# A four-layer-norm hybrid encoder on one core: GpSimd broadcasts the mLSTM's running maxima, a head's normalisation changes place, and the first and last pieces are cut smaller

## The chip, the core and the metric

The kernel runs on one core of one Trainium2 chip. The core has five engines that run side by side and wait for each other by semaphores: TensorE (PE, matrix products into PSUM; its weight loads are shown as PEld), VectorE (DVE), ScalarE (ACT), GpSimd (POOL) and SyncE (SP, which here only starts DMAs). The metric is the device time of one execution in microseconds (us). All times of instructions below are counted from the start of the profiled span.

## What is computed

The input is x, 256 tokens by 1024 features, float32. Two macaron layers follow each other; each is a SwiGLU block, a mixer and a second SwiGLU block, every one behind a residual with a factor and a layer norm:

```python
x = layer_norm(ALPHA * x + 0.5 * swiglu(x, w_in, w_out), g, b)
x = layer_norm(ALPHA * x + mixer(x), g, b)      # layer 0: mLSTM, layer 1: windowed attention
x = layer_norm(ALPHA * x + 0.5 * swiglu(x, w_in2, w_out2), g, b)
```

The mLSTM has 4 heads and runs in both directions over the tokens. In the reference it goes chunk by chunk; written out over all 256 tokens, direction d of head h weights the product of query t and key s by exp(u[s] - m[t]), where u is the input gate less the cumulated log forget gate and m[t] is the running maximum of u up to t (from the other end in the second direction). Sums of these weights, bounded below, divide the result; the two directions are added, each head is normalised over its 256 features, and a sigmoid gate and an output product follow. In 32-bit precision the kernel computes every product as three: each operand is split in a high part that TensorE takes exactly (float32r) and the rest, and high x high, high x low and low x high are added.

## The kernel before

**Stages.** Six stages run in order: ffn, mlstm, ffn, ffn, attn, ffn (the list `stages`, line 329). Tokens are handled as two tiles t of 128. `xt[t]` holds a token tile, `xT` its transpose in high and low parts.

**Weights.** The class `Weights` (line 147) streams all weights through a ring. A "word" is one load of 128x1024 floats by SP into `w_raw` (or `s_raw`), a "piece" is a word split by ACT into `w_hi` (`high`, line 214) and by DVE into `w_lo` (`low`, line 238). The ring has 10 pieces; `take` hands them out, `done` frees those used and lets the next ones be split. In the ffn stages the class `Paced` (line 52) keeps a running estimate of each engine's time and puts splits between the matmuls by it; in the mixers the places of the splits are written out by hand (`spare`, `W.done(0, n)`, lists such as `MP`). All engines work through their instructions in the program's order. Since every operation of PE, DVE and ACT passes through one helper, the profile shows them all under line 138; tiles tell them apart.

**Begin.** `ffn` with `start` (line 604) issues 14 transposes of the identity (`warm`), transposes the first half of `xt[0]` in 4 blocks into a PSUM bank `py`, splits it (DVE makes the high part there), splits piece 0 in two halves of 512 columns, and issues 8 more identity transposes. `first_mm` (line 629) then multiplies piece 0 and piece 1 in an order of its own.

**mLSTM.** `mlstm` (line 867) projects values, then gates. DVE makes the rows `cum`, `u` and the running maxima `pm` by scans (up to line 936). ACT and DVE split `pm` into `pn` (high part in partitions 0 to 63, low part in 64 to 127). In the loop over m and g (line 978) the queries and keys are projected, and after each of the four products `weights(h)` (line 961) makes the weights of one head: two matmuls of a column of `neg_id` with `pn` put -m[t] of each direction on all 128 partitions of a PSUM bank, ACT makes six exponentials of 128x128 from it with `u` as bias, and POOL sets the wrong side of the diagonal to zero by two selects. Then, for each head, `scores` multiplies queries, keys and weights, `mix` multiplies the result with the values, `divide` (line 1029) divides: ACT scales the first direction, DVE scales and adds the second. `combine` takes the head's mean and variance on DVE and lets POOL raise the variance to the power -1/2; `settle` (line 1054) subtracts and scales on DVE. `gate_out` multiplies by the sigmoid. The order of the heads is written out at line 1078: scores(h) with combine(h-2) inside, mix(h-1), divide(h-1), settle(h-2).

**End.** `tail` (line 559) ends every stage: all products of token tile 0, then tile 1. For tile 1 the output half o=1 does its first half of products, o=0 all, o=1 the rest (`order`, line 574). `Norm.half` adds a 512-column half to the residual and takes its statistics (`bn_stats`), `Norm.finish` aggregates them, lets POOL raise the variance to -1/2, and applies the norm in two DVE passes; in the last stage both go in cuts of 512 columns, and SP stores each cut.

Of the kernel before, what the change touches and what calls it, by code (L numbers as in the profile page):

```python
# [16 lines left out]
D = 1024  # L17
# [129 lines left out]
class Weights:  # L147
# [66 lines left out]
    def high(self):  # L214

        nc, i = self.nc, self.made
        p = self.plan[i]
        while self.half and (p["word"] not in self.raw or any(h[0] == p["needs"] for h in self.half)):
            self.low()
        while any(s_[0] == p["needs"] or p["word"] not in self.raw for s_ in self.sums):  # L220
            self.sum()
        if p["word"] not in self.raw:
            return False
        scale, raw = p["scale"], self.raw[p["word"]]
        hi = self.pool.tile([128, D], FR, name="w_hi", tag="w_hi", bufs=RING)
        if i == 0:
            for j in range(2):
                s_ = slice(j * 512, j * 512 + 512)
                nc.scalar.copy(hi[:, s_], raw[:, s_])
        elif scale is None:  # L230
            nc.scalar.copy(hi, raw)
        else:
            nc.scalar.activation(hi, raw, AF.Copy, scale=scale())
        self.half.append((i, hi))
        self.made += 1
        return True

    def low(self):
# [5 lines left out]
        lo = self.pool.tile([128, D], FR, name="w_lo", tag="w_lo", bufs=RING)  # L244
        if i == 0:
# [75 lines left out]
def trunk_kernel(ctx: ExitStack, tc: tile.TileContext, x, ffn_w_in, ffn_w_out, ln_g, ln_b, ml_w_in, ml_gate_b,  # L321
# [67 lines left out]
    for j, (kind, l, i, _) in enumerate(stages):  # L389
        if kind == "ffn":  # L390
# [7 lines left out]
            for c0 in (0, F):  # L398
                for a in range(4):
                    wide(wi, a * 256, c0)  # L400
            for g in range(GROUPS):
# [59 lines left out]
    neg_sink = consts.tile([128, 16], F32, name="neg_sink")  # L461
    neg_id = consts.tile([128, 64], FR, name="neg_id")

    def small_loads():
# [8 lines left out]
        nc.gpsimd.tensor_scalar(neg_sink, sink, -1.0, None, op0=OP.mult)  # L473
        nc.vector.scalar_tensor_tensor(neg_id, ident[:, 0:64], -1.0, ident[:, 64:128], op0=OP.mult, op1=OP.subtract)

# [52 lines left out]
    class Norm:  # L528
        def __init__(self, t, ca, eps, gb, last=False):
            self.t, self.ca, self.eps, self.gb, self.last = t, ca, eps, gb, last  # L530
            self.stats = state.tile([128, 2, 6], F32, name="stats", tag="stats", bufs=2)

        def half(self, h, y):
            z = xt[self.t][:, h * 512:(h + 1) * 512]
            nc.vector.scalar_tensor_tensor(z, z, self.ca, y, op0=OP.mult, op1=OP.add)
            nc.vector.bn_stats(self.stats[:, h], z)

        def finish(self, spare):
            mv = state.tile([128, 2], F32, name="mv", tag="mv", bufs=2)
            nc.vector.bn_aggr(mv, self.stats)  # L540
            rs = state.tile([128, 2], F32, name="rs", tag="rs", bufs=2)
# [7 lines left out]
            if len(cuts) == 1:  # L549
                W.done(0, spare)  # L550
            for s_ in cuts:
                nc.vector.scalar_tensor_tensor(z[:, s_], z[:, s_], rs[:, 1:2], self.gb[1][:, s_],
                                               op0=OP.mult, op1=OP.add)
                if self.last:
                    nc.sync.dma_start(out[0, tok(self.t), s_], z[:, s_])
            if len(cuts) > 1:
                W.done(0, spare)

    def tail(y, h, todo, first, norm, last, turn_at, between=None):

        def one(t, o, n):
            c, (i, w) = todo[t][n]
            mm3(y[t][o], h(c, t), pair(w, A, 0, slice(o * 512, o * 512 + 512)), first and n == 0, n == len(todo[t]) - 1)

# [11 lines left out]
        for j, (o, n) in enumerate(order):  # L576
            if j == full + turn_at:
                emit_x(0, last)
            one(1, o, n)
            if j >= half and (n < half) == (o == 0):  # L580
                W.done(todo[1][n][1][0] + 1, next(more))
            if n == full - 1:
                norm[1].half(o, y[1][o])
        norm[1].finish(1)
        W.done(most=TD[bound[0]])
# [6 lines left out]
    def ffn(l, i, n, pending, last):  # L592
        with ExitStack() as ph:
# [35 lines left out]
            def first_mm(ps, a):  # L629

                def mm(t, i, j):
                    for k in (2 * a, 2 * a + 1):
                        nc.tensor.matmul(ps[t], xT[i][:, k, tok(t)], pieces[a][j][:, k % 2], start=i == j == k == 0,
# [233 lines left out]
    def mlstm(l, n, pending, last):  # L867
        with ExitStack() as ph:
# [92 lines left out]
            def weights(h):  # L961
                w = tile_([128, 2, 3, 128], F32, "wt", bufs=4)
                pb = wbank((128, 2, S))
                for d in range(2):
                    r = 32 * d + h
                    sel = neg_id[:, r:r + 1].to_broadcast([128, 128])
                    nc.tensor.matmul(pb[:, d], sel, pn, start=True, stop=True)
                for sb in range(2):
                    nc.scalar.activation(w[:, 0, sb], pb[:, 0, tok(sb)], AF.Exp, bias=ucol[:, sb, h:h + 1])
                    nc.scalar.activation(w[:, 1, sb], pb[:, 1, tok(sb)], AF.Exp, bias=ucol[:, sb, 32 + h:33 + h])  # L970
                nc.scalar.activation(w[:, 0, 2], pb[:, 0, tok(1)], AF.Exp, bias=ucol[:, 0, h:h + 1])
                nc.scalar.activation(w[:, 1, 2], pb[:, 1, tok(0)], AF.Exp, bias=ucol[:, 1, 32 + h:33 + h])
                for d in range(2):
# [104 lines left out]
            for h in range(4):  # L1078
# [332 lines left out]
```

## Time and profile before

| what | value |
| --- | --- |
| median of 3 runs | 927.92 us (927.56 to 928.36) |
| the profiled execution itself | 928.32 us |
| its span, first to last instruction | 926.6 us |
| outside the span | 1.72 us |
| mean granted TensorE clock | 0.997 |
| PE / DVE / ACT / POOL busy | 99% / 85% / 59% / 11% of the span |
| DMA, mean over the span | 202 GB/s |

The profile is read by engines. A row of the timeline gives start, time, engine, line, operation, what it writes and reads, its shape and how many follow each other; in brackets the idle time of the engine just before and what ended it. A matmul row's end is modelled: matmuls overlap, and the distance between two starts tells what one costs. Where equal instructions are merged, the time is that from the first start to the last end.

### The profile page before, as it was taken

How to read it: one execution, taken by the hardware profiler on the slowest of the kernel's cores; microseconds unless marked ns; L12 is line 12 of the kernel's file. 1: busy time of each engine (PE TensorE's matmuls, PEld its weight loads, DVE VectorE, ACT ScalarE, POOL GpSimd, SP SyncE). 2: the span in 40 equal slices, each digit the busy share in tenths (PEclk: the TensorE clock that was granted, in tenths of full speed). 3: DMA queues.
4: the chain of work that ended last, by engine and by line, in shares of the span. 5: the costliest groups of instructions: out<-in, count | busy, mean ns of one | idle time of the engine just before them, and what ended most of it. 6: DMA issues, size and time to landing. Idle time of an engine off the chain costs nothing.

```text
span 926.6 us, 12512 instructions
## 1 busy us (share of the span) xinstructions
PE 916.5 (99%) x4506; PEld 767.3 (83%) x4506; DVE 785.4 (85%) x948; ACT 544.4 (59%) x766; POOL 98.1 (11%) x144
## 2 busy tenths in 40 slices
PE   9999999999999999999999999999999999999996
PEld 7888888889988888888888888888888888888885
DVE  5899997886699799988887899988868878998875
ACT  5656756347664548565636566565569555757460
POOL 0010103011111010101010101010435300110100
PEclk9999999999999999999999999999999999999998
DMA  8979774646535949685558597737434385969421
GB/s 280 356 180 334 216 246 74 229 133 199 188 108 188 344 112 345 166 304 137 160 176 323 144 330 210 269 69 227 156 122 133 101 273 195 274 194 346 122 86 45
DMA packets 98461, 187.54 MB, mean 202 GB/s; under 512 B 6720, under 2 KB 37456, under 8 KB 98400
## 3 DMA queue, kind: packets, MB, share of 16 engines
q1 hardware_dynamic: 91072, 173.04, 54.7%
q0 software_dynamic: 6752, 12.66, 8.6%
q10 hardware_dynamic: 576, 1.05, 0.3%
q8 instruction: 35, 0.57, 0.2%
q14 instruction: 26, 0.21, 0.1%
HBM read 185.68 MB, written 1.05 MB: 202 GB/s over the span
## 4 chain that ended last, share of the span: by engine, by line
PE 87%; DVE 8%; ACT 2%; issue 2%; DMA 1%; POOL 0%; SPq 0%; DVEq 0%; ACTq 0%; POOLq 0%
PE pw L138 56%; PE py L138 30%; DVE w_lo L138 3%; DMA s_raw<-in_ffn_w_in_dram 1%; DVE x L138 1%; ACT w_hi L138 1%; DVE s_raw L138 1%; DVE h L138 1%; DVE stats L138 0%; DVE wt L138 0%; ACT h L138 0%; DVE a_lo L138 0%; DVE hst L138 0%; DVE e L138 0%; DVE S L138 0%
## 5 line engine op out<-in xcount | busy, mean ns | idle before, releaser
L138 DVE TENSOR_TENSOR w_lo<-w_raw,w_hi 128x1024 fp32r<-128x1024 f32 (+1 forms) x237 | 281.8, 1219 | 24.7 <-ACT w_hi L138 22.4
L138 ACT CAST w_hi<-w_raw 128x1024 fp32r<-128x1024 f32 (+1 forms) x237 | 241.7, 1050 | 81.7 <-PE py L138 27.1
L138 PE MATMUL pw<-w_hi,xT_hi 128*128 128x512 f32 x560 | 221.6, 397 | 0.0
L138 PE MATMUL pw<-w_hi,xT_lo 128*128 128x512 f32 x560 | 218.0, 390 | 0.0
L138 PE MATMUL pw<-w_lo,xT_hi 128*128 128x512 f32 x560 | 217.4, 390 | 0.0
L138 ACT CAST w_hi<-s_raw 128x1024 fp32r<-128x1024 f32 x144 | 148.1, 1052 | 80.6 <-DVE s_raw L138 44.0
L138 DVE TENSOR_TENSOR w_lo<-s_raw,w_hi 128x1024 fp32r<-128x1024 f32 x144 | 173.0, 1220 | 22.4 <-ACT w_hi L138 21.9
L138 PE MATMUL py<-w_hi,h_hi 128*128 128x512 f32 x352 | 138.0, 392 | 0.0
L138 PE MATMUL py<-w_lo,h_hi 128*128 128x512 f32 x352 | 137.1, 390 | 0.0
L138 PE MATMUL py<-w_hi,h_lo 128*128 128x512 f32 x352 | 137.1, 390 | 0.0
L138 PEld LDWEIGHTS pw<-w_hi,xT_lo 128*128 128x128 f32 x560 | 105.0, 188 | 22.4
L138 PEld LDWEIGHTS pw<-w_lo,xT_hi 128*128 128x128 f32 x560 | 105.3, 188 | 21.0 <-DVE w_lo L138 0.4
L138 PEld LDWEIGHTS pw<-w_hi,xT_hi 128*128 128x128 f32 x560 | 105.0, 188 | 20.2 <-ACT xT_hi L138 0.2
L138 DVE TENSOR_TENSOR s_raw<-s_raw 128x1024 f32<-128x1024 f32 x72 | 87.2, 1221 | 1.0
L267 POOL DMA_DIRECT2D s_raw<-in_ffn_w_in_dram x24 | 29.2, 1215 | 511.8 <-DVE w_lo L138 469.4
L138 PEld LDWEIGHTS py<-w_hi,h_lo 128*128 128x128 f32 x352 | 66.1, 188 | 13.9
L138 PEld LDWEIGHTS py<-w_lo,h_hi 128*128 128x128 f32 x352 | 66.1, 188 | 13.8 <-DVE w_lo L138 0.3
L138 PEld LDWEIGHTS py<-w_hi,h_hi 128*128 128x128 f32 x352 | 66.1, 188 | 13.5
L138 PE MATMUL pw<-w_hi,S_hi 128*128 128x512 f32 x192 | 74.7, 389 | 0.0
L138 PE MATMUL pw<-w_lo,S_hi 128*128 128x512 f32 x192 | 74.7, 389 | 0.0
L138 PE MATMUL pw<-w_hi,S_lo 128*128 128x512 f32 x192 | 74.7, 389 | 0.0
L138 DVE TENSOR_TENSOR h_lo<-pw,h_hi 128x512 fp32r<-128x512 f32 x44 | 30.2, 688 | 24.4 <-ACT h_hi L138 24.3
(206 smaller groups left out, 1087.6 us busy)
## 6 DMA issues: line engine op xcount, KB each, us to landing
w_raw<-in_ffn_w_out_dram SPq DMA_DIRECT2D x88, 512.0 KB, 5.2
s_raw<-in_ffn_w_in_dram SPq DMA_DIRECT2D x72, 512.0 KB, 6.2
w_raw<-in_ffn_w_in_dram SPq DMA_DIRECT2D x56, 512.0 KB, 5.2
w_raw<-in_ffn_w_in_dram SPq DMA_DIRECT2D x96, 256.0 KB, 4.2
s_raw<-in_ffn_w_in_dram POOLq DMA_DIRECT2D x24, 512.0 KB, 6.0
w_raw<-in_ml_w_in_dram SPq DMA_DIRECT2D x24, 512.0 KB, 4.6
w_raw<-in_at_w_in_dram SPq DMA_DIRECT2D x12, 512.0 KB, 4.7
w_raw<-in_ml_w_out_dram SPq DMA_DIRECT2D x8, 512.0 KB, 4.0
```

Source lines behind the costliest of these rows:

```text
L138: r = f(out, *args, **kw)
L267: nc.gpsimd.dma_start(t.rearrange("p (k f) -> p k f", k=self.words[w]["k"]), v, accum_op=OP.add)
```

## The change

1. The mLSTM's maxima. `neg_id`, `pn` and the two matmuls per head go. Two DMAs issued by POOL copy the rows of `pm` to partitions 0, 32, 64, 96 of a new tile `most`; in `weights(h)` two POOL instructions `partition_broadcast` put each direction's row of 256 floats on all 128 partitions of the tile `wt`, in SBUF. ACT's six exponentials read that tile with scale -1 and write it in place, direction 0 first. In the built program POOL also gets an instruction that loads another instruction library ahead of the first broadcast and one that loads the usual one again after the last select.
2. A head's normalisation. `divide` takes a function `between`, called after ACT's scaling and before DVE's scale and add. `settle(h-2)` is called there instead of after `divide(h-1)`; the same for `settle(2)`, which now stands inside `divide(3)`, ahead of `combine(3)`.
3. The end. In the last stage's tile 1, half o=1 ends its first half of products with a sum of its own (`first`: residual plus sum, no statistics). The rest of that half is done in two quarters of 256 columns, each in its own PSUM bank; `quarter` adds and takes statistics of 256 columns. The last pass of the norm goes in cuts of 512, 256 and 256 columns, and ACT's queue instead of SP's issues the last store.
4. The begin. Word 0 is loaded by two DMAs of 256 KB. The first two 128-column blocks of `xt[0]` are transposed on their own into a bank `pw` and split first; the first four are then transposed into the bank `py` (of which blocks 2 and 3 are split, ACT making the high part), 6 identity transposes follow instead of 8. Piece 1 is also split in halves. `first_mm` uses piece 0 block by block, with the transposes of `xt[1]` after its first matmul instead of its second.

Apart from these places the order of instructions on every engine stays the same.

```diff
@@ high, low
-        if i == 0:
+        if i < 2:
...
@@ plan
-                    wide(wi, a * 256, c0)
+                    if j == c0 == a == 0:
+                        piece([two(wi, 0, 0)[:, k:k + 1] for k in range(2)], 2)
+                    else:
+                        wide(wi, a * 256, c0)
...
@@ class Norm
+        def first(self, h, y):
+            z = xt[self.t][:, h * 512:(h + 1) * 512]
+            nc.vector.scalar_tensor_tensor(z, z, self.ca, y, op0=OP.mult, op1=OP.add)
+
+        def quarter(self, h, q, y):
+            z = xt[self.t][:, h * 512 + q * 256:h * 512 + (q + 1) * 256]
+            nc.vector.tensor_add(z, z, y)
+            nc.vector.bn_stats(self.stats[:, h + q], z)
+            self.parts = 3
...
+            if self.parts == 3:
+                cuts = [slice(0, 512), slice(512, 768), slice(768, D)]
...
-                    nc.sync.dma_start(out[0, tok(self.t), s_], z[:, s_])
+                    (nc.scalar if n_ == 2 else nc.sync).dma_start(out[0, tok(self.t), s_], z[:, s_])
@@ tail
+            if last and j == full + half:
+                break
             one(1, o, n)
+            if last and j == half - 1:
+                norm[1].first(1, y[1][1])
...
+        if last:
+            for q in range(2):
+                yq = wbank((128, 256))
+                for n in range(half, full):
+                    c, (i, w) = todo[1][n]
+                    mm3(yq, h(c, 1), pair(w, A, 0, slice(512 + 256 * q, 768 + 256 * q)), n == half, n == full - 1)
+                norm[1].quarter(1, q, yq)
@@ ffn, start
-                to_xT(0, xt[0], ybank, (0,), nc.vector.tensor_copy)
+                early = wbank((128, 2, 128))
+                for k in range(2):
+                    nc.tensor.transpose(early[:, k], xt[0][:, tok(k)], ident)
+                split_evac(pair(xT, A, slice(0, 2), tok(0)), early, high=nc.vector.tensor_copy)
+                late = ybank((128, 4, 128))
+                for k in range(4):
+                    nc.tensor.transpose(late[:, k], xt[0][:, tok(k)], ident)
+                turned[0, 0] = late
                 W.split(1)
-                warm(8)
+                split_evac(pair(xT, A, slice(2, 4), tok(0)), late[:, 2:4])
+                warm(6)
@@ first_mm
-                mm(0, 0, 0)
                 if a == 0:
+                    mm(0, 0, 0, (0,))
                     to_xT(1, xt[1], ybank, (0,))
                     W.split(2)
-                mm(0, 1, 0)
+                    mm(0, 1, 0, (0,))
+                    mm(0, 0, 0, (1,))
+                    mm(0, 1, 0, (1,))
+                else:
+                    mm(0, 0, 0)
+                    mm(0, 1, 0)
@@ mlstm
-            pn = tile_([128, S], FR, "pn")
+            most = tile_([128, 2, S], F32, "most")
...
-            nc.scalar.copy(pn[0:64], pm)
-            nc.vector.tensor_sub(pn[64:128], pm, pn[0:64].bitcast(F32))
+            for d in range(2):
+                nc.gpsimd.dma_start(most[0:128:32, d], pm[32 * d:32 * d + 4])
...
-                pb = wbank((128, 2, S))
                 for d in range(2):
-                    r = 32 * d + h
-                    sel = neg_id[:, r:r + 1].to_broadcast([128, 128])
-                    nc.tensor.matmul(pb[:, d], sel, pn, start=True, stop=True)
-                for sb in range(2):
-                    nc.scalar.activation(w[:, 0, sb], pb[:, 0, tok(sb)], AF.Exp, bias=ucol[:, sb, h:h + 1])
-                    nc.scalar.activation(w[:, 1, sb], pb[:, 1, tok(sb)], AF.Exp, bias=ucol[:, sb, 32 + h:33 + h])
-                nc.scalar.activation(w[:, 0, 2], pb[:, 0, tok(1)], AF.Exp, bias=ucol[:, 0, h:h + 1])
-                nc.scalar.activation(w[:, 1, 2], pb[:, 1, tok(0)], AF.Exp, bias=ucol[:, 1, 32 + h:33 + h])
+                    nc.gpsimd.partition_broadcast(w[:, d, 0:2].rearrange("p b m -> p (b m)"), most[32 * h:32 * h + 1, d])
+                for d, blk in ((0, 1), (1, 0)):
+                    c = 32 * d + h
+                    nc.scalar.activation(w[:, d, 2], w[:, d, blk], AF.Exp, bias=ucol[:, 1 - blk, c:c + 1], scale=-1.0)
+                    for sb in range(2):
+                        nc.scalar.activation(w[:, d, sb], w[:, d, sb], AF.Exp, bias=ucol[:, sb, c:c + 1], scale=-1.0)
...
-            def divide(h):
+            def divide(h, between=None):
...
+                if between is not None:
+                    between()
...
-                    divide(h - 1)
+                    divide(h - 1, (lambda: settle(h - 2)) if h > 1 else None)
                 if h > 1:
-                    settle(h - 2)
                     spare()
...
-            divide(3)
+            divide(3, lambda: settle(2))
             combine(3)
-            settle(2)
             gate_out(0, 0)
```

More of the change, by code (lines that the diff above doesn't have):

```diff
@@ L244, in low @@
         lo = self.pool.tile([128, D], FR, name="w_lo", tag="w_lo", bufs=RING)
-        if i == 0:
+        if i < 2:
             for j in range(2):
@@ L461, in trunk_kernel @@
     neg_sink = consts.tile([128, 16], F32, name="neg_sink")
-    neg_id = consts.tile([128, 64], FR, name="neg_id")
     def small_loads():
@@ L473, in small_loads @@
         nc.gpsimd.tensor_scalar(neg_sink, sink, -1.0, None, op0=OP.mult)
-        nc.vector.scalar_tensor_tensor(neg_id, ident[:, 0:64], -1.0, ident[:, 64:128], op0=OP.mult, op1=OP.subtract)
     def mm3(o, l, r, start, stop, onto=False):
@@ L530, in __init__ @@
             self.t, self.ca, self.eps, self.gb, self.last = t, ca, eps, gb, last
-            self.stats = state.tile([128, 2, 6], F32, name="stats", tag="stats", bufs=2)
+            self.stats = state.tile([128, 32], F32, name="stats", tag="stats", bufs=2)[:, 0:18].rearrange("p (h s) -> p h s", h=3)
+            self.parts = 2
         def half(self, h, y):
@@ L536, in half @@
             nc.vector.bn_stats(self.stats[:, h], z)
+        def first(self, h, y):
[6 more added lines that the diff above has]
+            self.parts = 3
         def finish(self, spare):
             mv = state.tile([128, 2], F32, name="mv", tag="mv", bufs=2)
-            nc.vector.bn_aggr(mv, self.stats)
+            nc.vector.bn_aggr(mv, self.stats[:, 0:self.parts])
             rs = state.tile([128, 2], F32, name="rs", tag="rs", bufs=2)
@@ L550, in finish @@
                 W.done(0, spare)
-            for s_ in cuts:
+            if self.parts == 3:
+                cuts = [slice(0, 512), slice(512, 768), slice(768, D)]
+            for n_, s_ in enumerate(cuts):
                 nc.vector.scalar_tensor_tensor(z[:, s_], z[:, s_], rs[:, 1:2], self.gb[1][:, s_],
@@ L562, in one @@
             c, (i, w) = todo[t][n]
-            mm3(y[t][o], h(c, t), pair(w, A, 0, slice(o * 512, o * 512 + 512)), first and n == 0, n == len(todo[t]) - 1)
+            end = n == len(todo[t]) - 1 or last and t == o == 1 and n == len(todo[t]) // 2 - 1
+            mm3(y[t][o], h(c, t), pair(w, A, 0, slice(o * 512, o * 512 + 512)), first and n == 0, end)
         for o in range(2):
@@ L629, in first_mm, with mm @@
             def first_mm(ps, a):
-                def mm(t, i, j):
-                    for k in (2 * a, 2 * a + 1):
+                def mm(t, i, j, ks=(2 * a, 2 * a + 1)):
+                    for k in ks:
                         nc.tensor.matmul(ps[t], xT[i][:, k, tok(t)], pieces[a][j][:, k % 2], start=i == j == k == 0,
```

## The prediction

> **What bounds the kernel now.** I read the page's first part, then the windows, then PE's waits and the timeline of the three places that the change touches: the mLSTM (195 to 278 us), the end (from 917) and the begin (to 15).
>
> ```profile
> PE 916.5 (99%) x4506; PEld 767.3 (83%) x4506; DVE 785.4 (85%) x948; ACT 544.4 (59%) x766; POOL 98.1 (11%) x144
> ```
>
> PE is at work nearly all of the span, so a matmul that goes is time that goes, and other engines cost time only where PE waits for them. The windows show one place in the mLSTM where it does:
>
> ```profile
> 262.00:278.00 16.00, 15.29 (x70) 11.94 (x69) 15.25 (x26) 11.87 (x16) 2.32 (x2) 1.00 0.49 158
> ```
>
> The columns after the length are busy us of PE, PEld, DVE, ACT and POOL. DVE has 0.75 us free in 16, PE is idle 0.71: here DVE leads. PE's weight loads say for whom they waited between 195 and 300 us (total, times, longest), and the timeline shows one of these places:
>
> ```profile
> PEld py L138 <- DVE w_lo L138: 1.1, 2, 0.7
> PEld pw L138 <- issue: 0.7, 1, 0.7
> ```
> ```profile
> 268.48 0.60 PE L138 MATMUL pw<-ident,h 128*128 128x128 f32 x4
> 269.54 0.63 PE L138 MATMUL pw<-ident,h 128*128 128x128 f32 x4 [0.46 <-DVE h L138]
> ```
>
> Four transposes take about 0.44 from start to start (0.109 apart: 0.60 is three steps and the last one's 0.27), so the second four could begin at 268.92. They begin at 269.54: 0.62 lost, waiting for the gated heads `h`. The two waits for `w_lo` near 276 and 277 us add up to 1.1 at the weight loads, of which I count 0.8 as PE time lost. That makes some 1.4 us in which PE follows DVE.
>
> **The change part by part.**
>
> *Eight matmuls go.*
>
> ```profile
> 218.30 0.39 PE L138 MATMUL pw<-pn,neg_id 128*128 128x256 f32 x2
> 218.53 0.28 PE L138 MATMUL pw<-xT_hi,w_hi 128*128 128x256 f32 x1
> ```
>
> The two of one head hold PE for 218.53 - 218.30 = 0.23; four heads, 0.92. No PE wait lies between them, so this is on the path: -0.92, if what replaces them is in time. The ACT copy and the DVE subtraction that made `pn` go too; PE waits for neither, so I count them at 0.
>
> *What replaces them.* The rows of `pm` are ready when the scans end; POOL must then issue two small DMAs, load a library and broadcast twice before ACT comes to head 0's exponentials.
>
> ```profile
> 207.15 1.37 DVE L138 TENSOR_TENSOR_SCAN fm<-ones,ig 32x256 f32<-32x256 f32 x2
> ```
> ```profile
> 147.11 2.08 POOL L471 DMA_DIRECT2D gbias<-in_ml_gate_b_dram  x4 [0.29 <-POOL gbias L468]
> ```
> ```profile
> gbias<-in_ml_gate_b_dram POOLq DMA_DIRECT2D x4, 0.0 KB, 5.1
> ```
> ```profile
> 220.87 1.67 ACT L138 ACTIVATE wt<-pw,ucol 128x128 f32<-128x128 f32 x6
> ```
> ```profile
> 237.87 1.66 ACT L138 ACTIVATE wt<-pw,ucol 128x128 f32<-128x128 f32 x6
> 239.55 1.28 ACT L1077 ACT_TABLE_LOAD   x1
> ```
>
> Scans end at 207.15 + 1.37 = 208.52. POOL's small DMAs take 2.08 / 4 = 0.52 to issue and land 5.1 after issue: the second is issued by about 209.1 and lands at 213.7. Head 0's exponentials start at 220.87. So 11.8 us after the issue remain for the load and two broadcasts. No row shows the load in mid-run; it may take 0 to about 10 before anything is late. I take it as hidden. The Trainium skill (GPSIMD Engine Reference, 2.1 Instruction dispatch) puts the first call after such a load at about 6 us more with no row of its own; by it the sum here stays the same, as an estimate 5.8 us would be left for the broadcasts.
>
> The tight deadline is head 3's. POOL's rows of the selects and powers:
>
> ```profile
> 234.06 1.04 POOL L974 TENSOR_SCALAR_AFFINE_SELECT wt<-wt 128x256 f32<-128x256 f32 x2 [5.03 <-ACT wt L138]
> 238.82 1.03 POOL L974 TENSOR_SCALAR_AFFINE_SELECT wt<-wt 128x256 f32<-128x256 f32 x2 [3.71 <-ACT wt L138]
> 252.31 1.34 POOL L1049 TENSOR_TENSOR hrs<-hrs,mhalf 128x2 f32<-128x2 f32 x1 [12.45 <-DVE hrs L138]
> 257.59 1.34 POOL L1049 TENSOR_TENSOR hrs<-hrs,mhalf 128x2 f32<-128x2 f32 x1 [3.94 <-DVE hrs L138]
> 262.00 1.60 POOL L1049 TENSOR_TENSOR hrs<-hrs,mhalf 128x2 f32<-128x2 f32 x1 [3.08 <-DVE hrs L138]
> 266.05 0.72 POOL L1049 TENSOR_TENSOR hrs<-hrs,mhalf 128x2 f32<-128x2 f32 x1 [2.44 <-DVE hrs L138]
> ```
> ```profile
> L974 POOL TENSOR_SCALAR_AFFINE_SELECT wt<-wt x8: 403/541/864, 221.8 to 239.5; 128x256 f32<-128x256 f32 x8
> ```
> ```profile
> L1155 POOL TENSOR_TENSOR dist<-fwd,back 128x512 f32<-128x512 f32 x1 | 2.1, 2141 | 0.1
> ```
>
> Head 2's selects end at 235.10, head 3's exponentials start at 237.87: 2.77, less 0.23 (one pair of matmuls fewer between the two heads) and 0.2 (the second select now waits for all six exponentials): 2.35 for two broadcasts, 1.17 each. A broadcast writes 128x256; the selects write as much in 0.40 to 0.86 (minimum, median and maximum are in the row, in ns); the power on two columns takes 0.72 to 1.60, and the longest row of POOL outside DMAs, an add of 512 columns, 2.14. Bounds 0.4 and 2.1, taken 0.7, nearest the selects: in time. Queued behind a late broadcast stand, on ACT, the table load, head 0's `a_hi` and with it `mix(0)` on PE; on POOL, the selects. The library is loaded back between 239.85 and the power at 252.31: 12.5 us, hidden.
>
> A row speaks against it: DVE's last `w_lo` before 238.82,
>
> ```profile
> 238.00 1.23 DVE L138 TENSOR_TENSOR w_lo<-w_raw,w_hi 128x1024 fp32r<-128x1024 f32 x1 [0.24 <-ACT w_hi L138]
> ```
>
> runs to 239.23, and the two selects end 0.62 after it though the first began at 238.82. The Trainium skill (SBUF — State Buffer, Who interferes with whom) says that a VectorE instruction with two SBUF inputs and a GpSimd one that reads SBUF hold a shared port as an exclusive lock, and the later blocks until the other is done; the row agrees, and the rule would put one `w_lo` (1.2) into the time between two heads. At 0.7 each, broadcasts and one such block take 2.6 of 2.35: 0.25 late, less than ACT's slack at 241 us.
>
> *Settle moves into divide.* Head 3's turn:
>
> ```profile
> 258.48 0.18 DVE L138 RECIPROCAL den<-den 128x4 f32<-128x4 f32 x1
> 259.26 0.88 DVE L138 SCALAR_TENSOR_TENSOR h<-py,den,h 128x256 f32<-128x256 f32 x2 [0.60 <-ACT h L138]
> 260.05 0.73 DVE L138 TENSOR_SCALAR h<-h,hmv,hrs 128x256 f32<-128x256 f32 x2
> ```
>
> DVE idles 0.60 between the reciprocal (ends 258.66) and the add, waiting for ACT's scaling; the two settles come after, starting 260.05 and holding the queue to 260.69 or so (0.64). Put into the gap, they wait for POOL's power, which ends at 257.59 + 1.34 = 258.93: settle starts at about 258.98 instead of filling the gap from 258.70, the add at 258.98 + 0.65 = 259.63 instead of 259.26. So 0.37 is lost ahead of the add and 0.64 won behind it: -0.27. The same relation holds at the other two places (powers from 252.31 and 262.00), so DVE's chain gains 0.8 in all. The new wait is DVE's for POOL; the adds and statistics stand behind it, as priced.
>
> That chain ends in the waits of PE above. DVE's work at 240 us starts from PE's scores, so it moves 0.92 earlier with them, and 0.8 more by the settles: it delivers at 277 us some 1.72 earlier. PE could gain up to 0.92 + 1.4 = 2.3 there, so DVE decides: **-1.72**. From 281 us on PE runs through to the end and carries it.
>
> *The end.*
>
> ```profile
> 917.81 0.69 DVE L138 BATCH_NORM_STATS2 stats<-x 128x6 f32<-128x512 f32 x1
> 919.12 0.69 DVE L138 SCALAR_TENSOR_TENSOR x<-x,py 128x512 f32<-128x512 f32 x1 [0.62 <-PE py L138]
> 919.85 0.69 DVE L138 BATCH_NORM_STATS2 stats<-x 128x6 f32<-128x512 f32 x1
> 920.58 0.21 DVE L138 BATCH_NORM_AGGREGATE mv<-stats 128x2 f32<-128x12 f32 x1
> 920.82 0.15 DVE L138 TENSOR_SCALAR rs<-mv 128x1 f32<-128x1 f32 x1
> 920.89 1.40 DVE L138 SCALAR_TENSOR_TENSOR x<-x,mv,ln_g 128x512 f32<-128x512 f32 x2
> ```
> ```profile
> 922.21 1.41 DVE L138 SCALAR_TENSOR_TENSOR x<-x,rs,ln_b 128x512 f32<-128x512 f32 x2
> ```
> ```profile
> 917.57 0.39 PE L138 MATMUL py<-w_hi,h_hi 128*128 128x512 f32 x1
> 917.79 0.39 PE L138 MATMUL py<-w_lo,h_hi 128*128 128x512 f32 x1
> ```
> ```profile
> L138 DVE BATCH_NORM_STATS2 hst<-h 128x6 f32<-128x256 f32 x8 | 3.0, 416 | 0.0
> ```
>
> Now 919.12 (PE done) to 920.58 is 1.46 for an add and statistics of 512 columns. Statistics of 256 take 0.42, and I take the same for the add. PE's last nine matmuls, 0.22 to 0.23 from start to start, become 18 of 0.12 (as in the pair above): 0.12 later, done at 919.21. The first quarter's add starts when DVE is through with the statistics of 917.81, at 918.42, its statistics at 918.87; the second's add at 919.25, statistics 919.70, aggregation 920.15 instead of 920.58: -0.43. The last pass then costs three starts instead of two, 512, 256, 256 columns: its end moves from 923.62 - 0.43 = 923.19 to 923.24. The last store is of half the size and from ACT's queue, which is free. The stores take 2.0 to land:
>
> ```profile
> out_dram<-x SPq DMA_DIRECT2D x4, 256.0 KB, 2.0
> ```
>
> With 0 to 0.25 less for half the bytes: **-0.4 to -0.6, taken -0.5**.
>
> *The begin.*
>
> ```profile
> 4.49 1.06 PE L138 MATMUL py<-ident,x 128*128 128x128 f32 x4
> 5.34 1.81 PE L138 MATMUL py<-ident 128*128 128x128 f32 x8
> 6.91 0.71 PE L138 MATMUL pw<-w_hi,xT_hi 128*128 128x512 f32 x2
> ```
>
> PE is held by 4 + 8 transposes until the first product at 6.91. Afterwards it is 2 + 4 + 6: as many. All that comes earlier (half a weight, half a transpose) waits for the same point: **0**, with ±0.25 either way, for a short wait of PE near 14 us may go or grow.
>
> **Sum.** -1.72 - 0.5 = -2.2. The profiled execution takes 928.32 (span 926.6 and 1.72 around it) and would take 926.1; it lies 0.40 over the median of 927.92, so the median comes to **925.7**.
>
> **The rivals.** *Only the matmuls pay.* If the settles wait longer for POOL than the gap (its 1.34 blocked by DVE, as above), DVE's chain gains nothing, and -0.92 - 0.5 gives 926.5. For it: three of four powers take 1.34 or more, the free one 0.72. Against: their ends already stand in the sum.
>
> *GpSimd becomes the bound: slower.* Between two heads POOL needs 0.45 for a select, two broadcasts b, a blocked 1.2, 0.1 of waits and ACT's 1.67: 3.42 + 2b, against (237.87 - 220.87) / 3 = 5.67, now 5.44. Three steps late by 2b - 2.02 each, less 0.5 of slack at ACT's `a_hi`, are PE's loss. It eats the whole 2.2 from b = 1.46; at b = 2.1, 3 x 2.18 - 0.5 = 6.0, and the time is 931.7. For it: the port, and the add's 2.14; against: the selects' 0.52. Between b = 1.1 and 1.46 the time is between 925.7 and 927.9.
>
> *More is won.* If the store of half the size lands much sooner and the wait at 14 us goes, another 0.5 to 0.8: 924.9 to 925.2.
>
> **How the numbers follow.** Forecast 0.50 (its own range 925.1 to 926.3); only the matmuls 0.18; GpSimd a little late 0.10; GpSimd the bound, 928 and more, 0.10; more won 0.12. The range 924.9 to 927.9 leaves out the slow end and part of the fast: about 0.16. What a measurement can tell from no change is 0.2%, 1.86 us. Faster than 926.06 are most of the forecast and the fast case: 0.56. Slower than 929.78: 0.09. Between: 0.35.
>
> **What would show it.** Right: no `pn` rows; broadcasts of 0.4 to 1.1 that end before ACT reaches the exponentials; no idle of ACT ahead of `wt`; DVE's idle before `h<-py,den,h` down from 0.60, filled by settles; the second four transposes of `h` right behind the first; PE's product after the last `w_lo` wait near 275.4 instead of 277.1; aggregation 1.1 us, not 1.5, behind PE's last product. Wrong: ACT waiting for POOL at `wt`, DVE's `w_lo` longer than 1.22 beside a broadcast, a first product later than 6.91, or a last store that takes over 2.0 from ACT's queue.

## The result and the profile after

The changed kernel takes 936.39 us in the median (935.78 to 936.80, 6 runs), the kernel before 928.14 (6 runs): ratio 1.0087, 95% interval 1.0074 to 1.0100. Forecast were 925.7 us and a range up to 927.9; the change is slower by 8.25 us. The rival that ends slower, GpSimd as the bound, is not what happened either. The first part of the page after:

```profile
PE 924.8 (99%) x4507; PEld 768.1 (82%) x4507; DVE 785.5 (84%) x952; ACT 545.5 (58%) x767; POOL 107.6 (12%) x154
```

Before, PE was busy 916.5 us with 4506 instructions in a span of 926.6; now 924.8 with 4507 in 934.8. So the 8.2 us are not idle time: PE waits no longer than before, and its instructions take longer. The granted clock is the same (mean 0.997 before, 0.998 after). The groups of PE's instructions say which; the last columns are busy us and mean ns of one. First the kernel before, then the changed one:

```profile
L138 PE MATMUL pw<-w_hi,xT_hi 128*128 128x512 f32 x560 | 221.6, 397 | 0.0
L138 PE MATMUL py<-w_hi,h_hi 128*128 128x512 f32 x352 | 138.0, 392 | 0.0
L138 PE MATMUL pw<-w_lo,S_hi 128*128 128x512 f32 x192 | 74.7, 389 | 0.0
```
```profile
L138 PE MATMUL pw<-w_hi,xT_hi 128*128 128x512 f32 x560 | 222.2, 398 | 0.0
L138 PE MATMUL py<-w_hi,h_hi 128*128 128x512 f32 x349 | 138.9, 398 | 0.0
L138 PE MATMUL pw<-w_lo,S_hi 128*128 128x512 f32 x192 | 75.9, 395 | 0.0
```

Products with `xT` take 1 ns more, those with `h` and `S` 6 ns. (These means are longer than what one product costs, since matmuls overlap.) `h` and `S` are the stationary operands of the second half of every ffn stage. What one costs is seen from the starts in the timeline, here thirteen products with `S` in the middle of the kernel before and of the changed one (first and last row):

```profile
618.42 0.39 PE L138 MATMUL pw<-w_hi,S_hi 128*128 128x512 f32 x1
...
621.14 0.39 PE L138 MATMUL pw<-w_hi,S_hi 128*128 128x512 f32 x1
```
```profile
623.94 0.39 PE L138 MATMUL pw<-w_hi,S_hi 128*128 128x512 f32 x1
...
626.73 0.39 PE L138 MATMUL pw<-w_hi,S_hi 128*128 128x512 f32 x1
```

Twelve steps take 2.72 us before and 2.79 after: 227 against 232 ns. No engine is late and no row shows a wait.

What moved is where these tiles lie in SBUF. `neg_id` (64 floats, 256 bytes per partition) lay ahead of the weights and is gone, so that all behind it lies 256 lower, which leaves every place modulo 256 as it was. And the change holds a line of which neither its description above nor the prediction speaks, since no instruction follows from it:

```diff
-            self.stats = state.tile([128, 2, 6], F32, name="stats", tag="stats", bufs=2)
+            self.stats = state.tile([128, 32], F32, name="stats", tag="stats", bufs=2)[:, 0:18].rearrange("p (h s) -> p h s", h=3)
```

Two buffers of 48 bytes, laid out 64 apart, become two of 128 bytes: all that lies behind `xT`, `h` and `S` with it, lies 128 higher. By the built program's table of addresses `w_hi`, `w_lo`, `xT`, `h` and `S` all lie at 96 modulo 256 in the kernel before; in the changed one `w` and `xT` still do, and `h` and `S` lie at 224.

**The parts that the prediction priced.** In the mLSTM, the changed kernel has no `pn`, and POOL's groups and first rows read:

```profile
L1004 POOL PARTITION_BROADCAST wt<-most x8 | 7.9, 1055 | 6.0 <-issue 5.7
```
```profile
211.04 1.28 POOL L978 DMA_DIRECT2D most<-fm  x2 [12.57 <-DVE fm L138]
218.00 1.85 POOL L1004 PARTITION_BROADCAST wt<-most  x2 [5.68 <-issue]
```

The eight broadcasts take 1.0 us in the mean, where 0.7 was taken for each (bounds 0.4 and 2.1); further below it is shown that this mean mixes two kinds. Between the two DMA issues and the first broadcast POOL is idle for 5.7 us. The DMAs of `most` have landed by 213.97; for the last 4.0 the profile shows nothing that POOL waits for, which leaves the library. The Trainium skill (GPSIMD Engine Reference, 2.1 Instruction dispatch) gives about 6 us for the first call after a load, and the trace agrees (5.7). The eight matmuls, the gates and all that leads to the last transposes of `h` can be timed between two rows, first of the kernel before and then of the changed one:

```profile
198.22 0.28 PE L138 MATMUL pw<-xT_hi,gw_hi 128*128 128x256 f32 x1
...
280.40 1.03 PE L138 MATMUL pw<-ident,h 128*128 128x128 f32 x8
```
```profile
201.11 0.28 PE L138 MATMUL pw<-xT_hi,gw_hi 128*128 128x256 f32 x1
...
270.60 1.03 PE L138 MATMUL pw<-ident,h 128*128 128x128 f32 x8
281.65 1.03 PE L138 MATMUL pw<-ident,h 128*128 128x128 f32 x8
```

82.18 before, 80.54 after: 1.64 won, of 1.72 forecast. The eight transposes of `h` that stood in two rows with 0.62 lost between them are one row. So the mechanism there is as predicted, and the loss lies in stages whose instructions the change does not touch.

### The profile page after: what moved, and what is told of

The parts are those of the page before. It is cut to its first block, busy times and chain, and to the rows that moved or that the text cites. A ratio compares the mean times of both kernels' runs of the same rounds, so it can differ in the third digit from the quotient of the medians.

```text
span 934.8 us, 12540 instructions
## 1 busy us (share of the span) xinstructions
PE 924.8 (99%) x4507; PEld 768.1 (82%) x4507; DVE 785.5 (84%) x952; ACT 545.5 (58%) x767; POOL 107.6 (12%) x154
## 4 chain that ended last, share of the span: by engine, by line
PE 97%; DVE 1%; DMA 0%; ACT 0%; issue 0%; DVEq 0%
PE pw L138 64%; PE py L138 34%; DMA x<-in_x_dram 0%; DVE w_lo L138 0%; DVE x L138 0%; DVE stats L138 0%; ACT xT_hi L138 0%; ACT w_hi L138 0%; DVE q_lo L138 0%; ACT q_hi L138 0%; DVEq L1444 0%; DVE mv L138 0%; DVE rs L138 0%; DVEq L138 0%
```

## The experiments

Each kernel was timed beside the kernel before on the same chip; times are medians. Theory ADDRESS: the places of `h` and `S` modulo 256 cost the time. Rival GPSIMD: the broadcasts, the library and their waits cost it.

**1. The changed kernel with `h` and `S` put back.** An unused tile behind `xT`:

```diff
           state.tile([128, 8, S], FR, name="xT_lo", tag="xT_lo"))
+    state.tile([128, 32], F32, name="pad", tag="pad")
```

> The changed kernel with an unused tile of 128 bytes per partition behind xT, so that h_hi, h_lo and S again lie at 96 modulo 256 bytes, as w_hi and w_lo do (in the changed kernel they lie at 224). Theory ADDRESS (the matmuls whose stationary operand lies 128 bytes off the moving one's place modulo 256 start 232 instead of 227 ns after each other; 1584 of them x 5.7 ns = 9.0 us, and nothing else lost): 926 to 927 us, and the distance of py<-w,h_hi and pw<-w,S_hi back at 227. Rival GPSIMD (broadcasts of 1.0 us each, the library load and their waits cost the 8 us): unchanged, 936. Rival BOTH: in between, 930 to 934.

Measured: 927.0 us against 928.5, ratio 0.9983 (0.9973 to 0.9992). PE's busy time on the page and the groups are back at the values of before, though the broadcasts are in it (the page of the kernel before counts 3 x (352 + 192) = 1632 products with `h` and `S`, not the 1584 of the expectation):

```profile
PE 915.4 (99%) x4507; PEld 767.1 (83%) x4507; DVE 785.3 (85%) x952; ACT 545.3 (59%) x767; POOL 106.4 (11%) x154
```
```profile
L138 PE MATMUL py<-w_hi,h_hi 128*128 128x512 f32 x349 | 136.9, 392 | 0.0
L138 PE MATMUL pw<-w_lo,S_hi 128*128 128x512 f32 x192 | 74.7, 389 | 0.0
```

**2. The kernel before with the same tile, and nothing else.**

> The kernel before with the same unused tile of 128 bytes behind xT and no other edit: h and S move to 224 modulo 256, w and xT stay at 96. Theory ADDRESS: 928 + 9 to 10 = 937 to 938 us, distance of the matmuls with h and S 232 ns instead of 227, and those with q in the attention 227 to 229 instead of 232. Rival GPSIMD: an unused tile costs nothing, 928.

Measured: 938.03 against 928.5, ratio 1.0104 (1.0089 to 1.0119): 9.5 us for 128 bytes that nothing reads. The attention's `q`, which lies at 224 before, comes to 96 with it, and its products go from 232 ns to 228 to 229. GPSIMD falls.

**3. The same 128 bytes ahead of the weights** (`consts.tile([128, 32], F32, name="padc")` behind `neg_sink`), so that all tiles move together.

> The kernel before with an unused tile of 128 bytes ahead of all weights: w, xT, h and S all move to 224 modulo 256, and keep their places relative to each other. Theory ADDRESS, RELATIVE form (stationary against moving): 928, distances as before. Theory ADDRESS, ABSOLUTE form (224 is bad in itself): the matmuls with xT become slow too, some 3300 x 5.5 ns = 18 us: 946. Rival GPSIMD: 928.

Measured: 929.49 against 928.5, ratio 1.0007 (0.9998 to 1.0017), `h_hi` at 392 ns and `S` at 389. No place is bad in itself; the relation counts.

**4 and 5. Smaller distances:** the tile of experiment 2 with 64 and with 32 bytes.

> The kernel before with an unused tile of 64 bytes behind xT: h and S at 160 modulo 256, w at 96. Theory ADDRESS, if the cost grows with the distance: something between 928 and 937, at half way about 932; if only 128 apart collides: 928; if every place but the same is slow: 937. Rival GPSIMD: 928.

> The kernel before with an unused tile of 32 bytes behind xT: h and S at 128 modulo 256 bytes, w at 96. If every place other than the same is slow, as 64 and 128 bytes off were: 232 to 234 ns for the products with h and S, 938 us. If 32 bytes still fall in the same line: 227 ns, 928.5.

Measured: 938.69 against 928.5 (1.0107, 1.0092 to 1.0122) and 938.77 against 928.77 (1.0109, 1.0095 to 1.0123). The cost does not grow with the distance; 32 bytes off is as bad as 128.

**6. Which operands?** `w_lo` alone moved by 128, with a second tile ahead of `xt` so that the rest keeps its place:

```diff
+        if i == 0:
+            self.pool.tile([128, 32], F32, name="padw", tag="padw", bufs=1)
         lo = self.pool.tile([128, D], FR, name="w_lo", tag="w_lo", bufs=RING)
...
+    state.tile([128, 32], F32, name="pad", tag="pad")
     xt = [state.tile([128, D], F32, name=f"x{t}", tag=f"x{t}") for t in range(2)]
```

> The kernel before with w_lo alone at 224 modulo 256 bytes (unused tiles ahead of w_lo and behind it), w_hi, xT, h and S at 96. Theory MOVING (the moving operand of one product and the stationary one that is loaded beside it must lie at the same place modulo 256): the products with w_lo become slow, 227 to 232 ns, those with w_hi stay at 227: about 1230 x 5.5 ns = 6.8 us, 935. Rival STATIONARY (only the places of stationary tiles count, relative to each other or to something else): 928.

Measured: 945.14 against 928.77, ratio 1.0180 (1.0165 to 1.0196), 16.4 us. Both forms miss. The products with `w_hi`, whose two operands lie alike, are slow too:

```profile
L138 PE MATMUL pw<-w_hi,xT_hi 128*128 128x512 f32 x560 | 224.4, 402 | 0.0
L138 PE MATMUL pw<-w_hi,S_hi 128*128 128x512 f32 x192 | 76.3, 397 | 0.0
L138 PE MATMUL pw<-w_lo,S_hi 128*128 128x512 f32 x192 | 75.8, 395 | 0.0
```

**7 and 8. The distance by itself.** A kernel that only copies x to the output and issues groups of 48 products from two moving tiles mA, mB and two stationary tiles sA, sB; A and B lie 128 (then 256) bytes apart modulo 256 (512), and no other engine and next to no DMA runs beside the products:

```
RUNS = [("A", "A", 48), ("A", "A", 48), ("A", "B", 48), ("B", "B", 48), ("B", "A", 48), ("AB", "A", 48), ...
...
    nc.tensor.matmul(p, T[ss[i % len(ss)]][:, i % 8], M[ms[i % len(ms)]][:, h:h + 512], start=i == 0, stop=i == n - 1)
```

> A kernel with matmuls alone (its output is x itself, nothing of the reference is computed): twelve groups of 48 products, 128x128 by 128x512 in float32r, with nothing beside them on other engines. mA and sA lie at 128 modulo 256 bytes, mB and sB at 0. Groups: moving/stationary A/A twice, A/B, B/B, B/A, then moving A,B in turn with A; A,B,A with A; A with A,B in turn; A,B with A,B; A,B with B,A; A,B,A with A,A,B; A/A. Theory PAIR-NEXT (the moving tile of one product and the stationary tile loaded meanwhile for the next must lie alike): A/A and B/B 227 ns, A/B and B/A 232, A,B with A between (229.5), A,B with A,B all slow, A,B with B,A all fast. Theory PAIR-SAME (moving and stationary of the same product): A,B with A,B fast, A,B with B,A slow. Theory SET (all tiles in play must lie alike): every mixed group slow, 232 or more. Rival TRAFFIC (it takes the writes of other engines or DMAs beside): 227 everywhere.

> The same probe with 256 bytes between the A and the B tiles in place of 128, so that all lie alike modulo 256 (but not modulo 512). All theories of 256 bytes: 227 ns in every group. If the period is 512: the same groups slow as in the probe with 128.

With 128 bytes between A and B, PE's timeline has one row for a group that changes no tile (start, us from first start to last end). The first A/A group is left out: its first steps are 427 ns and more, in both probes.

```profile
19.02 11.05 PE L39 MATMUL pcb<-mA,sA 128*128 128x512 f32 x48
29.90 11.32 PE L39 MATMUL pcc<-mA,sB 128*128 128x512 f32 x48
41.06 11.10 PE L39 MATMUL pcd<-mB,sB 128*128 128x512 f32 x48
51.99 11.32 PE L39 MATMUL pce<-mB,sA 128*128 128x512 f32 x48
63.15 0.40 PE L39 MATMUL pcf<-mA,sA 128*128 128x512 f32 x1
```

From start to start over 48: A/A 227 ns, A/B 232.5, B/B 228, B/A 232.5. With 256 bytes all are equal:

```profile
19.72 11.04 PE L39 MATMUL pcb<-mA,sA 128*128 128x512 f32 x48
30.60 11.04 PE L39 MATMUL pcc<-mA,sB 128*128 128x512 f32 x48
41.48 11.04 PE L39 MATMUL pcd<-mB,sB 128*128 128x512 f32 x48
52.36 11.04 PE L39 MATMUL pce<-mB,sA 128*128 128x512 f32 x48
63.24 0.39 PE L39 MATMUL pcf<-mA,sA 128*128 128x512 f32 x1
```

So the period is 256 bytes (128 apart is slow, 256 apart is not), it needs no traffic beside (TRAFFIC falls), and it is between the stream of the moving operand and that of the weights. In the mixed groups the mean distances are, in the order of the list, 230.1 (moving A,B with stationary A), 233.2 (A,B,A with A), 232.3 (A with A,B), 228.4 (A,B with A,B), 229.9 (A,B with B,A) and 231.4 ns (A,B,A with A,A,B). None is as fast as 226.7, whatever pairs are formed: PAIR-NEXT wanted 227 for A,B with B,A, and PAIR-SAME 227 for A,B with A,B. SET holds in its sign, not in its amount: not every mixed group reaches 232. The rule within mixed groups stays open.

**9 and 10. The first and the second part alone** on the kernel before: the broadcasts; the settles.

> The kernel before with the first part alone: GpSimd's broadcasts for TensorE's matmuls with neg_id and pn; h and S keep their places relative to w. The prediction's step: -0.92 between the gates (198 us) and the first scores (239 us), GpSimd and ACT not late although a broadcast takes 1.0 instead of the 0.7 that was taken and the six exponentials 2.0 instead of 1.66; the DVE wait near 275 us grows by less: time 0.5 to 1.0 below the kernel before. Theory START: PE's first instruction at 1.71 instead of 1.45, as in all kernels with this part so far; 0.25 later without effect on the first product. Rival GPSIMD BOUND: ACT's waits for the broadcasts give the 0.92 back, no change or slower.

> The kernel before with the second part alone, the settles inside divide. The prediction's step: DVE's chain 0.8 shorter between 252 and 272 us. Theory WORD (a weight word lands too late for ACT's split to follow, so PE gets only part of it): PE gains 0.3 to 0.5 by 282 us, time 0.3 to 0.5 lower, with ACT waiting for the DMA of a w_out word near 274 us. Rival ALL: PE gains 0.8. Rival NOTHING (the new waits for POOL's power eat the gap): 0.

Measured: broadcasts 927.93 against 928.77 (0.9992, 0.9983 to 1.0001), settles 927.46 against 928.77 (0.9991, 0.9982 to 0.9999). Between the same two rows as above, `b_bcast` takes 280.68 - 199.16 = 81.52 and `b_settle` 280.79 - 199.51 = 81.28 of before's 82.18: -0.66 and -0.90. The medians hardly tell either from no change; these rows do. The settles bring all of the 0.8 that they were priced at (ALL, not WORD). The broadcasts bring 0.90 at the scores (40.11 us after the gates against 41.01), of which 0.24 is lost again. Nearly all of that goes at one place, where DVE's add waits 0.88 for ACT's scaling instead of the 0.60 of before:

```profile
259.50 0.88 DVE L138 SCALAR_TENSOR_TENSOR h<-py,den,h 128x256 f32<-128x256 f32 x2 [0.88 <-ACT h L138]
```

Counted from the gates, DVE is 0.97 earlier than before ahead of this row and 0.70 behind it; what held ACT there is not shown. A weight word that lands after ACT is ready for it takes another 0.04:

```profile
274.85 1.15 ACT L138 ACTIVATE w_hi<-w_raw,gcol 128x1024 fp32r<-128x1024 f32 x1 [0.41 <-DMA w_raw<-in_ml_w_out_dram]
```

In experiment 1 the same wait is 0.86:

```profile
274.30 1.15 ACT L138 ACTIVATE w_hi<-w_raw,gcol 128x1024 fp32r<-128x1024 f32 x1 [0.86 <-DMA w_raw<-in_ml_w_out_dram]
```

and there it decides: DVE is 1.78 earlier than before ahead of the word's `w_lo` and 1.29 earlier at it, and PE's part of the 1.72 is 280.15 - 199.24 = 80.91, so -1.27.

**11 to 13. The begin and the end.** From experiment 1: the last store from SP; in `ap_sp_old` the begin of before as well; in `ap_sp_q` a tile of 128 bytes ahead of the attention's `q`; and the new begin alone on the kernel before.

```diff
-                    (nc.scalar if n_ == 2 else nc.sync).dma_start(out[0, tok(self.t), s_], z[:, s_])
+                    nc.sync.dma_start(out[0, tok(self.t), s_], z[:, s_])
```

> The changed kernel with h and S back in place (the tile of 128 bytes), and the last store issued by SP as before instead of by ACT. Theory CLOSING (with the store on ACT's queue SP waits first, of all its closing waits, for the store that lands last, and eight more waits of 0.06 us each stand behind it: 0.49 us): last store's landing to the end of the span 1.25 us instead of 1.74, the time 0.4 to 0.5 below the 927.0 of the kernel with ACT's store, 926.5. Rival QUEUE (ACT's queue is as good, the 0.43 lost at the end lie elsewhere): 927.0 and 1.7 us after the landing.

> As the kernel before it (h and S in place, last store from SP), and the begin of the kernel before the change: no early transposes, piece 1 not halved, word 0 in one load. Theory BEGIN (the new begin costs 0.3 to 0.9 us: in its profile the first product came at 7.52 instead of 6.91, and 0.31 more was lost near 62 us): 0.3 to 0.9 faster than with the new begin, 925.6 to 926.2, first product at 6.8 to 6.9 and no loss near 62 us. Rival LANDING (the begin differs from run to run with the landing of x, 4.5 to 5.3 us, whatever the code): same time as with the new begin within 0.3.

> The changed kernel with h and S in place, last store from SP, and a second unused tile of 128 bytes ahead of q in the attention, so that q's stationary tiles lie at 96 modulo 256 bytes as well. Theory ADDRESS: the 96 products with q start 227 to 228 ns after each other instead of 232 to 233, 96 x 5 ns = 0.5 us less than without the tile: 926.0. Rival (q's slow distance has another cause, such as the sums beside it): 232 ns stay, 926.5.

> The kernel before with the new begin alone (layout of h and S not touched). Theory BEGIN: 0.3 to 0.9 us above the kernel before, first product after 7.2 us, and a wait of PE of 0.2 to 0.4 for w_lo near 62 us. Rival LANDING and the prediction: the same as the kernel before within 0.25.

Measured: `ap_sp` 926.97 against 928.69 (0.9980, 0.9971 to 0.9989); `ap_sp_old` 927.92 (0.9992, 0.9983 to 1.0000); `ap_sp_q` 927.06 (0.9988, 0.9979 to 0.9997); `b_begin` 928.38 (1.0001, 0.9992 to 1.0010). The old begin is no faster: LANDING. Over the profiles the first transposes of x start between 4.49 and 5.28 us with the old begin and between 5.05 and 5.20 with the new one, the first product between 6.1 and 7.5 and between 6.4 and 7.5. The wait near 62 us is real, in `b_begin` too,

```profile
61.83 0.50 PE L138 MATMUL py<-w_lo,h_hi 128*128 128x512 f32 x1 [0.26 <-DVE w_lo L138]
```

but it does not show in the time. With `q` in place its products start 228 to 230 ns after each other instead of 232 to 233 (`py<-w_lo,q_hi` goes from 394 to 391 ns in the groups); 0.3 us over 96 products is below what the medians tell apart.

The end is the step that gains nothing. In experiment 1 DVE is done and the last store issued like this:

```profile
921.28 1.54 DVE L138 SCALAR_TENSOR_TENSOR x<-x,rs,ln_b 128x512 f32<-128x512 f32 x3
922.05 0.81 SPq L571 DMA_DIRECT2D out_dram<-x  x2
922.85 0.35 ACTq L138 DMA_DIRECT2D out_dram<-x  x1
```

By the DMA records the last byte lands 1.74 us before the span's end; in the kernel before 1.25. After its last issue SP waits for the semaphores of all DMAs one by one, some 0.06 apart, in a fixed order. The DMAs take eight of these in turn. Before, the last store had the last one of the list; with one DMA more at the begin and one more at the end it has an early one, and the others are gone through after it. So CLOSING as it was put, with ACT's queue as the cause, falls: from SP's queue, in `ap_sp`, the tail is 1.67, the value that QUEUE named. The count of DMAs would explain it, whichever engine issues them; `b_begin`, whose end is that of before and which has one DMA more, has 1.67 as well, and 7.91 from PE's end to the span's end where the kernel before has 7.49.

**14. The last store's semaphore moved to the end of the list**, by issuing the first store of token tile 0 in 7 pieces:

```diff
-                    nc.sync.dma_start(out[0, tok(self.t), s_], z[:, s_])
+                    m_ = 7 if self.t == 0 and n_ == 0 else 1
+                    for q_ in range(m_):
+                        c_ = slice(s_.start + q_ * 512 // m_, s_.start + (q_ + 1) * 512 // m_) if m_ > 1 else s_
+                        nc.sync.dma_start(out[0, tok(self.t), c_], z[:, c_])
```

> The changed kernel with h and S in place, the last store from SP, and the first store of token tile 0 in 7 pieces in place of 1, so that the last store's semaphore is the last of the eight that DMAs take in turn, and so the last that SP waits for in its closing waits. Theory CLOSING: landing of the last store to the end of the span 1.25 to 1.35 us instead of 1.67 to 1.74, time 0.35 to 0.45 below the 927.0 of its kin. Rival: the tail stays at 1.7.

Measured: the tail is 1.31 us and PE's end to the span's end 7.12 instead of 7.48 in `ap_sp`; CLOSING holds. The time is 926.30 against 928.35, ratio 0.9982 (0.9973 to 0.9991). It is below both kernels of the change, and cannot be told from experiment 1 or `ap_sp` by its time; the 0.36 is read from the traces.

## Why the prediction was wrong

The step that failed stands at the end of its part on the settles: "From 281 us on PE runs through to the end and carries it." It took each matmul that the change leaves alone to cost what it cost before. It did run through, at 232 instead of 227 ns for the products with `h` and `S`: +9.5 us by experiment 2, from a line whose price I had put at nothing by not looking at it. Nor did it wait for 281 us: `h` and `S` stand in the first stage as well, and the gates start at 201.11, where they start between 197.9 and 199.5 in the kernels whose `h` and `S` lie like the weights. A term for the layout was missing, and no rival had one.

Step by step, for what was priced:

- *Eight matmuls, -0.92.* Right: from the gates to the first scores 41.01 us before, 40.10 in experiment 1.
- *GpSimd in time.* Right, but a broadcast alone was priced too high, and the block by DVE's `w_lo`, which the prediction weighed beside its sum, is real. The eight broadcasts of experiment 1 (minimum, median and maximum in ns), and head 3's two with the `w_lo` beside them:

```profile
L1005 POOL PARTITION_BROADCAST wt<-most x8: 543/648/1634, 216.8 to 236.5; - x8
```
```profile
236.14 2.04 POOL L1005 PARTITION_BROADCAST wt<-most  x2
236.54 1.23 DVE L138 TENSOR_TENSOR w_lo<-w_raw,w_hi 128x1024 fp32r<-128x1024 f32 x1 [1.58 <-ACT w_hi L138]
```

The first of the two takes 0.55 us. The second starts just behind a `w_lo`, takes 1.63 and ends 0.41 after it, while the `w_lo` keeps its usual 1.22. The seven traces with broadcasts agree: each of the 28 that start while a `w_lo` runs ends 0.41 to 0.42 after that one, so that it takes between 0.75 and 1.64; the other 28 take 0.54 to 0.55. So the 1.0 is a mean of free and blocked broadcasts, not the price of one. The six exponentials take 2.0 where they took 1.66; their input is now in SBUF instead of PSUM and they write it in place, which was not priced, and which of the two costs the time was not tried. All is in time, since direction 0 comes first: in `b_bcast` ACT starts at 238.16, before the second broadcast ends at 238.27, and the fourth exponential, the first that reads it, starts at 239.05. In experiment 1 no idle time of ACT stands ahead of head 3's:

```profile
238.22 2.00 ACT L138 ACTIVATE wt<-wt,ucol 128x128 f32<-128x128 f32 x6
```

- *Settles, -0.8 on DVE's chain.* Right, and by the way that was given: the three places bring 0.26, 0.30 and 0.31. In experiment 1 the wait for POOL's power stands ahead of the settles, and the adds no longer wait:

```profile
258.73 0.73 DVE L138 TENSOR_SCALAR h<-h,hmv,hrs 128x256 f32<-128x256 f32 x2 [0.30 <-POOL hrs L1089]
259.38 0.87 DVE L138 SCALAR_TENSOR_TENSOR h<-py,den,h 128x256 f32<-128x256 f32 x2
```

- *"So DVE decides: -1.72."* Right in amount in the changed kernel (-1.64) and in `ap_sp_q` (279.00 - 198.59 = 80.41, -1.77); the other kernels with both parts give -1.47 (`ap_sp`), -1.74 (`ap_sp_old`) and -1.79 (`ap_tail7`), and in experiment 1 a weight word's landing decides instead (-1.27). What is late next was a DMA, which I had not listed.
- *The end, -0.5.* Wrong. In experiment 1 the aggregation starts 0.95 us after PE's end instead of 1.49, as forecast (0.43 earlier with PE 0.12 later). Against these 0.54 stand 0.17 more from the aggregation to the last store's issue, with three cuts in place of two, and 0.49 more in the closing waits. A store of half the size is signalled as late as a whole one, 2.0 us after its issue; by the DMA records its last byte lands 0.06 sooner. PE's end to the span's end: 7.49 before, 7.55 in experiment 1. The prediction had no term for what the program waits for after the last store.
- *The begin, 0.* Right within what the medians tell (1.0001, 0.9992 to 1.0010), and in part by luck: its one DMA more costs 0.42 at the end of `b_begin`, which no term had. A first product later than 6.91 was named as a sign of being wrong; it comes at 7.23 in the changed kernel, but the old begin gives 6.1 to 7.5 as well, so that it tells nothing.

Without the layout's term the forecast of -2.2 stands against -1.5 in experiment 1, which is -1.27 or more in the mLSTM and nothing at the end.

## What to carry to other kernels

When PE is at work all the time, count the matmuls that a change leaves alone: 5.5 ns on 1632 of them outweigh eight that are removed. Look at every tile whose size changes, not only at instructions: list the addresses of the matmuls' operands in both built programs and compare them modulo 256 bytes; if they came apart, an unused tile puts them back. Where the last DMA has landed earlier and the kernel has not ended earlier, look at what the program waits for at its end, and in which order.

## What the runs showed of the hardware

- Matmuls of 128x128 by 128x512 in float32r start 226.7 ns after each other when moving and stationary tiles lie alike modulo 256 bytes in their partitions, and 232.5 when they lie 128 apart, with nothing else running (the probe). The Trainium skill (SBUF — State Buffer, Who interferes with whom) gives TensorE two read ports, one for the moving operand and one for the weights, independent of each other; the distances measured here say that the two are not independent in time, and the measurement decides.
- After a change of place the fast distance comes back only after some products: in the probe's group B/B the first ten steps were 224 to 236 ns, and all that follow 226 or 227.
- A broadcast of one row of 256 floats to 128 partitions by GpSimd takes 0.55 us; one that starts while a `w_lo` of 1.22 us runs on DVE ends 0.41 to 0.42 after it (28 of 28 in seven traces), and the `w_lo` is no longer for it. The first one after the library's load starts 5.7 to 6.4 us after POOL has issued the DMAs ahead of it.
- PE's first instruction starts at 1.71 us instead of 1.45 in every kernel with the broadcasts. Why was not tried; whether the first product comes later for it cannot be told (6.6 to 7.5 in these kernels, 6.1 to 7.5 in the others).
